# Row sums of the first modulation by column-tiled products, and a re-ordered handover from router to experts

## The chip, the cores and the metric

The kernel runs on one core of one Trainium2 chip. The metric is device time in microseconds (us) of one execution. A core has five engines that are meant here: PE (TensorE, the matrix unit; its weight loads are shown apart as PEld), DVE (VectorE), ACT (ScalarE), POOL (GpSimd) and SP (SyncE, which here only issues DMAs and reads a few integers into registers). Each works through its own instructions in order; they wait for each other on semaphores.

## The reference

Two layers on x of 512 tokens by 1024 channels (f32). Each layer has a token mixer (layer 0: an mLSTM, layer 1: differential attention) and a mixture of experts, each behind a normalisation whose scale and shift come from a vector c:

```python
c_act = silu(c)
for l in range(2):
    mod = c_act @ w_ada[l] + b_ada[l]                 # 1024 -> 6 * 1024
    sh1, sc1, g1, sh2, sc2, g2 = split(mod, 6)
    h = rms(x, norm1[l]) * (1 + sc1) + sh1
    y = mlstm(h) if l == 0 else diff_attention(h)     # first step: h @ w_in
    x = x + g1 * y
    h = rms(x, norm2[l]) * (1 + sc2) + sh2
    x = x + g2 * grouped_moe(h)
```

`grouped_moe` routes each token to one of 4 groups of 4 experts and to the two best experts in it; an expert is 1024 -> 2 x 512, silu(gate) * up, 512 -> 1024. The weights of all 16 experts of a layer are 100 MB in f32.

## The kernel before

Everything is written for a scheduler that is given the instructions in program order and orders each engine's stream by a simulated time; a tile belongs to a tag of a pool with so many buffers, and a new tile of that tag waits until an old one is read for the last time. Two such tags matter: `whi` (3 buffers) and `wlo` (2 buffers) hold the high and low parts into which `split` (line 218) cuts weights, the high part written by ACT, the low part by DVE or POOL. Products that must be exact are made of three products of such parts (`triple`).

**Start.** x is loaded and normalised (`normed_T`). The first two of the six parts of `mod` (shift and scale of layer 0) are made in halves of 512 columns by `ada_half(hf, where)` (line 272). For each of the two parts it loads two blocks of w_ada (128 partitions x 4 x 512, 1 MiB each); ACT multiplies two of a block's four row groups by their column of c, DVE multiplies and adds the others (lines 283 to 289). `sums` then turns the 128 x 512 sums with PE, reduces them with DVE along the free axis (`column_sums`, line 258) and adds b_ada. The first half's result lets `modulated(xT, h, 0)` write h for the first four of eight row groups, and so starts the products of q (`proj_cols`, `strip`), which need `split` weights qk0s0, qk0s2 for the first half and qk0s4, qk0s6 for the second. The second half (`rest_of_h`, line 491) is woven into the first steps of q. Other parts of `mod` are made later, block by block, on ACT and POOL (`ada`, line 237); they share four load buffers (tag `raw`) with the mixer's weights.

**Router.** For each tile t of 128 tokens `tile_done` (line 1009) has POOL multiply x by a row (two pieces of 512 columns), ACT sum its squares, and `rstd_of` (line 317) make the reciprocal root of the mean square, a power, on POOL. `turn` and `logits` make the router's logits on PE; `rows` finishes the normalised rows on DVE and stores them to DRAM from POOL's queue. `choose`, `place` and `order` pick the experts, the place of each token in its expert's list, `count`, the rank of the 13 dynamic experts by count (`rk`), how many blocks are past the planned room (`past`), and `ids`, the experts in rank order. `weigh` has PE make the gates per slot (`psg`), and `by_rank` (line 1137) permutes lists and gates by rank.

**Handover and experts.** `moe` (line 1239) gathers expert 0's rows (`rows_in`, an indirect DMA on POOL), then `overflow` (line 1455) holds a loop over `past` blocks; with these inputs it makes no trip, but all engines go through its entry and exit together. Behind it the rows of expert 0 are turned on PE, written as parts xh and xl by ACT and DVE, and `gate_up` cuts each weight block and multiplies. Experts 0 to 8 run on up to 128 rows with `triple`, the last seven on 64 rows in plain f32 with two column groups of PE side by side (line 1275). The weights come through 15 buffers; the first 14 (layer 0) or 15 (layer 1) loads are issued ahead of the loop. A load for a dynamic expert has its address from a register that SP reads from `ids` (line 1215).

## Time and profile before

| | us |
|---|---|
| median of 3 runs | 1259.03 |
| lowest, highest | 1256.88, 1259.57 |
| profiled execution, own time | 1258.35 |
| its span | 1256.4 |

| engine | busy us | share of the span |
|---|---|---|
| PE | 1113.8 | 89% |
| PEld | 816.6 | 65% |
| DVE | 873.6 | 70% |
| ACT | 698.2 | 56% |
| POOL | 381.4 | 30% |

The mean granted TensorE clock is 0.93 of full (2.4 GHz; the lower level is 1.2 GHz). In round numbers the span is: start to 33 us, layer 0's mixer to 290, its router to 319, its experts to 590, layer 1's mixer to 948, its router to 978, its experts to the end. A share of busy time is a mean over stages with different limits, so each stage is read by itself: the table by stretches gives busy time of each engine there, the timeline gives each instruction with its start, its length and what its engine waited for. A wait for several things is put down to the last of them.

### The profile page before, as it was taken

To read this page: it belongs to the slowest core of one execution; us is meant where nothing else is said; L and a number is where in the kernel's file an instruction comes from. 1 tells how busy PE (TensorE), PEld (TensorE's weight loads), DVE (VectorE), ACT (ScalarE), POOL (GpSimd) and SP (SyncE) were. 2 spreads that over 40 slices of the span, in tenths; PEclk is the share of its full clock that TensorE was granted. 3 is DMA by queue.
4 is the path that set the end of the run, shared out by engine and by line. 5 is a ranking of instruction groups with operands and counts; after the bars stand their busy time and mean duration, and the time that the engine had idled before them with its cause. 6 is when DMAs were issued, how large, how long until landed. Compare 5 with 4: busy or idle time off the path is not lost. (4 is left out here: it accounts for less than half of the span.)

```text
span 1256.4 us, 16914 instructions
## 1 busy us (share of the span) xinstructions
PE 1113.8 (89%) x5714; PEld 816.6 (65%) x5714; DVE 873.6 (70%) x1622; ACT 698.2 (56%) x1164; POOL 381.4 (30%) x273
## 2 busy tenths in 40 slices
PE   3899999987899999995799999888897999999994
PEld 2577877766777875332688877665576787875331
DVE  6955878887788994006767889795776798993006
ACT  5456675442788884112656666565552788884110
POOL 2544572452211111102351455551332211101100
PEclk7799999997899999998799999897896899999997
DMA  9777662183899999998233335320464799999995
GB/s 349 248 246 282 243 233 101 66 341 143 289 390 383 377 390 365 397 409 272 94 102 117 119 127 175 131 73 1 168 248 167 268 386 375 387 384 366 391 410 202
DMA packets 105196, 320.79 MB, mean 255 GB/s; under 512 B 12674, under 2 KB 25098, under 8 KB 105105
## 3 DMA queue, kind: packets, MB, share of 16 engines
q1 hardware_dynamic: 96272, 298.67, 64.6%
q0 software_dynamic: 8832, 20.99, 4.6%
q8 instruction: 47, 0.77, 0.2%
q14 instruction: 45, 0.36, 0.1%
HBM read 309.66 MB, written 20.45 MB: 263 GB/s over the span
## 5 line engine op out<-in xcount | busy, mean ns | idle before, releaser
L253 POOL TENSOR_TENSOR acc<-acc,ada 128x1024 f32<-128x1024 f32 x58 | 151.0, 2604 | 89.4 <-ACT ada L252 36.7
L1275 PE MATMUL pge<-we,xfe 128*64 128x512 f32 x448 | 103.2, 599 | 2.5 <-DMA we<-in_moe_w_gu_dram 2.5
L1247 POOL DMA_INDIRECT xg<-h2d,lstd x26 | 26.4, 1016 | 235.8 <-PE xTe L380 156.3
L1284 DVE TENSOR_TENSOR acte<-acte,pge 128x256 f32<-128x256 f32 x14 | 5.9, 420 | 125.0 <-ACT acte L1283 125.0
L252 ACT ACTIVATE ada<-ada,cact 128x1024 f32<-128x1024 f32 x58 | 64.7, 1143 | 30.8 <-DMA ada<-in_w_ada_dram 30.7
L1275 PEld LDWEIGHTS pge<-we,xfe 128*64 128x64 f32 x448 | 29.3, 136 | 55.6 <-issue 48.2
L877 ACT ACTIVATE p<-p,mx 128x128 f32<-128x128 f32 (+3 forms) x64 | 35.6, 557 | 42.5 <-DVE mx L876 42.5
L1302 PE MATMUL pye<-we,aTe 128*64 128x512 f32 x224 | 54.1, 624 | 1.7 <-ACT aTe L1291 1.1
L320 POOL TENSOR_TENSOR qrs<-qrs,nhalf 128x4 f32<-128x4 f32 x32 | 36.7, 1151 | 61.2 <-DVE qrs L319 47.8
L870 PE MATMUL s<-kTb,qTb 64*128 64x128 f32 (+3 forms) x128 | 44.8, 530 | 11.1 <-DVE mx L873 10.4
L465 POOL TENSOR_TENSOR wo<-wo,grow 128x1024 f32<-128x1024 f32 x16 | 40.1, 2523 | 30.2 <-DVE wos102l L222 15.1
L1302 PEld LDWEIGHTS pye<-we,aTe 128*64 128x64 f32 x224 | 16.4, 144 | 36.5 <-issue 31.9
L873 DVE CUSTOM_DVE_ANT_0 p<-s,maskW 128x128 f32<-128x128 f32 (+3 forms) x64 | 29.8, 484 | 12.6 <-PE s L870 5.5
L1283 ACT ACTIVATE acte<-pge 128x256 f32<-128x256 f32 x14 | 5.4, 384 | 54.6 <-PE pge L1275 54.6
L1333 PE MATMUL pcf<-yo,self 64*128 64x512 f32 x64 | 18.9, 636 | 17.6 <-DVE acte L1284 15.9
L1314 ACT ACTIVATE yo<-pye,twins 128x512 f32<-128x512 f32 x10 | 6.9, 687 | 48.7 <-PE pye L1302 48.7
L1315 POOL DMA_INDIRECT yd<-yo,rows x10 | 10.0, 998 | 78.1 <-ACT yo L1314 77.5
L844 DVE TENSOR_TENSOR qrow<-qrow,qrs 128x256 f32<-128x256 f32 x32 | 26.5, 828 | 7.9 <-POOL qrs L320 7.6
L1291 ACT ACTIVATE aTe<-aTe 128x256 f32<-128x256 f32 x14 | 5.4, 383 | 45.5 <-PE aTe L1289 45.5
L1398 POOL DMA_INDIRECT yd<-yoe,lstd x12 | 14.7, 1225 | 52.4 <-ACT yoe L1503 50.7
L320 POOL TENSOR_TENSOR ors<-ors,nhalf 128x2 f32<-128x2 f32 (+1 forms) x12 | 12.0, 999 | 58.9 <-DVE ors L319 25.0
L250 DVE SCALAR_TENSOR_TENSOR acc<-ada,cact,acc 128x1024 f32<-128x1024 f32 x12 | 15.4, 1281 | 19.4 <-POOL acc L253 16.5
(2545 smaller groups left out, 3963.2 us busy)
## 6 DMA issues: line engine op xcount, KB each, us to landing
we<-in_moe_w_gu_dram SPq DMA_DIRECT2D x128, 1024.0 KB, 9.4
we<-in_moe_w_down_dram SPq DMA_DIRECT2D x64, 1024.0 KB, 10.5
ada<-in_w_ada_dram SPq DMA_DIRECT2D x48, 1024.0 KB, 5.2
yk<-yd SPq DMA_DIRECT2D x16, 512.0 KB, 10.0
wo<-in_a_w_out_dram SPq DMA_DIRECT2D x4, 1024.0 KB, 4.9
wo<-in_b_w_out_dram SPq DMA_DIRECT2D x4, 1024.0 KB, 6.2
x<-in_x_dram SPq DMA_DIRECT2D x4, 512.0 KB, 5.2
qk0w<-in_a_w_in_dram SPq DMA_DIRECT2D x2, 1024.0 KB
```

The lines of the kernel that those rows point to most:

```text
L252: A.activation(raw[:, k], raw[:, k], AF.Copy, scale=cact[:, kt:kt + 1])
L253: G.tensor_tensor(acc, acc, raw[:, k], op=ALU.add)
L320: G.tensor_tensor(r, r, nhalf[:, 0:ncol], op=ALU.pow)
L465: G.tensor_tensor(raw[:, k], raw[:, k], grow, op=ALU.mult)
L844: V.tensor_tensor(row3, row3, r[:, :, None].to_broadcast([P, ng, BHD]), op=ALU.mult)
L870: T.matmul(ps[:, 0:n], part(qTs, h)[q0:q0 + BHD, j * P:(j + 1) * P], part(kTs, h)[q0:q0 + BHD, 0:n], start=True, stop=True)
L873: V.tensor_tensor_reduce(p[:, 0:n], ps[:, 0:n], maskW[:, S - n:S], scale=1.0, scalar=NEG, op0=ALU.add, op1=ALU.max, accum_out=mx[:, cc:cc ...
L877: A.activation(p[:, 0:n], p[:, 0:n], AF.Exp, scale=0.125, bias=mx[:, cc:cc + 1], accum_out=mx[:, 2 + cc:3 + cc])
L1247: G.indirect_dma_start(out=xg[0:n], out_offset=None, in_=h2d[:, :], in_offset=bass.IndirectOffsetOnAxis(ap=itok[0:n], axis=0), bounds_chec ...
L1275: T.matmul(pgu[hf * CS:(hf + 1) * CS].rearrange("p (g c) -> p g c", g=2), x[:, kt], w[:, :, hf], start=kt == 0, stop=kt == NK - 1))
L1302: T.matmul(py[hf * CS:(hf + 1) * CS], aT[:, k, ch * CS:(ch + 1) * CS], w[:, 0, hf * 512:(hf + 1) * 512], start=ch + k == 0, stop=ch + k == 2))
L1333: ordered(T.matmul(banks[hf], sel[at, t], yo[at], start=first, stop=last))
```

## The change

Five edits. (1) `ada_half` no longer scales and adds on ACT and DVE: a zero-padded copy of c (`cpad`, 128 x 8 x 32, in a buffer of tag `wlo`) is the weight of 128 x 32 f32 products, four for each block on four column groups of PE, summed in one PSUM tile over both blocks; the 128 x 512 result is copied out (once by DVE, once by ACT) and its four useful rows are summed by one-column products with a column of ones. (2) In `tile_done` the square and the power come first; the first POOL product of a tile is issued behind the power of the tile before, the second behind its own. (3) `by_rank`, now with the making of `ids` and the add of the second `psg`, is called behind the overflow loop and after the gather of expert 1's rows; `cols`, `rank` and `byrank` move to a pool that lives on. (4) The first two weight splits of expert 0 are made ahead of the loop. (5) The loop's body uses plain f32 products, without splitting weights.

```diff
+    cpad = wsp.tile([P, NK, 32], F32, tag="wlo", name="cpad", bufs=N_LO)
+    V.memset(cpad, 0.0)
+    V.tensor_copy(cpad[:, :, 0], cact)
...
     def ada_half(hf, where):
-        accs = []
+        rows = []
         for i, j in enumerate((1, 0)):
-            acc = room[0].tile([P, D], F32, tag="acc", name=f"acc0{j}{hf}", bufs=2)
-            accs.append(acc)
+            ps = (y_tile, t_tile)[hf](f"rowada{j}{hf}")
             for ch in range(2):
                 raw = load(wk(w_ada[0, ch * 512:(ch + 1) * 512, j * D + hf * 512:j * D + (hf + 1) * 512]), 4, 512,
                            f"ada0{j}{hf}{ch}", where[2 * i + ch])
-                c = [cact[:, ch * 4 + k:ch * 4 + k + 1] for k in range(4)]
-                for n in range(2):
-                    A.activation(raw[:, n] if ch else acc[:, n * 512:(n + 1) * 512], raw[:, n], AF.Copy, scale=c[n])
-                if ch:
-                    V.tensor_tensor(acc, acc, raw[:, 0:2].rearrange("p a n -> p (a n)"), op=ALU.add)
-                for n in range(2):
-                    part = acc[:, n * 512:(n + 1) * 512]
-                    V.scalar_tensor_tensor(part, raw[:, 2 + n], c[2 + n], part, op0=ALU.mult, op1=ALU.add)
-            V.tensor_tensor(acc[:, 0:512], acc[:, 0:512], acc[:, 512:], op=ALU.add)
+                for k in range(4):
+                    T.matmul(ps[k * 32:(k + 1) * 32], cpad[:, ch * 4 + k], raw[:, k], start=ch == 0, stop=ch == 1)
+            row = room[0].tile([P, 512], F32, tag="acc", name=f"row0{j}{hf}", bufs=2)
+            if i:
+                A.activation(row, ps, AF.Copy)
+            else:
+                V.tensor_copy(row, ps)
+            rows.append(row)
         def sums():
-            cs = small.tile([P, 2, 4], F32, tag="cs", name=f"cs0{hf}", bufs=2)
-            column_sums(cs, accs[::-1], f"psada0{hf}")
+            ps = t_tile(f"psada0{hf}")
+            for i, row in enumerate(rows[::-1]):
+                for k in range(4):
+                    T.matmul(ps[:, i * 4 + k:i * 4 + k + 1], row[:, k * P:(k + 1) * P], ones_f[:, 0:1], start=True,
+                             stop=True)
...
     def rstd_of(src, ncol, count, name, pows=[]):
-        G.tensor_tensor(r, r, nhalf[:, 0:ncol], op=ALU.pow)
+        pows.append(G.tensor_tensor(r, r, nhalf[:, 0:ncol], op=ALU.pow))
...
         def tile_done(t):
+            ss = small.tile([P, 1], F32, tag="ss", name=f"sse{l}{t}", bufs=4)
+            A.activation(xT.rearrange("p k t -> p (k t)"), xt[t], AF.Square, accum_out=ss)
+            before = pows[-1:]
+            rst[t] = rstd_of(ss, 1, D, f"re{l}{t}", pows)
             for n in range(2):
                 cols = slice(n * 512, (n + 1) * 512)
-                G.tensor_tensor(h2[:, cols], xt[t][:, cols], arow[:, cols], op=ALU.mult)
-            ss = small.tile([P, 1], F32, tag="ss", name=f"sse{l}{t}", bufs=4)
-            A.activation(xT.rearrange("p k t -> p (k t)"), xt[t], AF.Square, accum_out=ss)
-            rst[t] = rstd_of(ss, 1, D, f"re{l}{t}")
+                with tc.issue_after((pows[-1] if n else before[0]).ins) if n or before else nullcontext():
+                    G.tensor_tensor(h2[:, cols], xt[t][:, cols], arow[:, cols], op=ALU.mult)
...
          def order():
-            later(1, lambda: by_rank(perm, work[:, 2 * N2:5 * N2]))
...
-        def by_rank(perm, moved):
+        def by_rank(work):
+            V.tensor_tensor(sg, sg, held[0], op=ALU.add)
...
             V.tensor_tensor(perm, rk[:, None, :].to_broadcast(square), eidx[:, 0:ND, None].to_broadcast(square),
                             op=ALU.is_equal)
             V.tensor_tensor(turned, perm[0:1], eidx[0:1, None, dyn].to_broadcast([1, ND, ND]), op=ALU.mult)
             V.tensor_reduce(idf, turned, axis=AX.X, op=ALU.add)
             V.tensor_copy(ids, idf)
...
-                    hi, lo = split(raw(k), 1, D, f"gus{nm}{kt}")
+                    hi, lo = ready.pop(0) if ready else split(raw(k), 1, D, f"gus{nm}{kt}")
...
                 def product(ps, xs, w):
                     for kt, x in enumerate(xs):
                         raw = part(w, kt)
                         for n in range(2):
+                            T.matmul(ps[n], x, raw[:, n * 512:(n + 1) * 512], start=kt == 0, stop=kt == len(xs) - 1)
...
         rows_in(0)
+        ready = [split(fetch.ready[0][:, k:k + 1], 1, D, f"guse0{k}") for k in range(2)]
         overflow()
         fetch.more(N_LAST[l], lst[:, 0, 0:1])
         cur = start("e0")
         for hf in range(2):
             turn(cur, xgs[0], hf, "e0")
         rows_in(1)
+        by_rank(yo_tile("work"))
         gate_up(cur, weights, (0, 1), "e0")
```

## Rows read from the trace of the kernel before

**Rows 1.** The page: busy tenths of PE, granted clock, 40 slices of 31.4 us.

```profile
PE   3899999987899999995799999888897999999994
...
PEclk7799999997899999998799999897896899999997
```

**Rows 2.** Stretches: length, busy us (instructions) by engine, clock, DMA share, GB/s.

```profile
13.00:34.00 21.00, 3.00 (x13) 2.37 (x14) 18.32 (x27) 11.10 (x18) 5.34 (x3) 0.57 1.05 388
60.00:230.00 170.00, 163.62 (x772) 131.24 (x771) 122.04 (x222) 103.79 (x161) 81.10 (x36) 1.00 0.59 205
350.00:400.00 50.00, 50.00 (x234) 40.17 (x233) 46.15 (x46) 41.92 (x50) 6.12 (x6) 1.00 1.02 390
```

**Rows 3.** Timeline of the start: start, length (us), engine, line, operation, [idle before, releaser].

```profile
20.98 1.33 ACT L283 ACTIVATE ada<-ada,cact 128x512 f32<-128x512 f32 x2 [1.36 <-DMA ada<-in_w_ada_dram]
...
24.83 2.40 POOL L222 TENSOR_TENSOR qk0s0l<-qk0w,qk0s0h 128x1024 fp32r<-128x1024 f32 x1 [12.67 <-ACT qk0s0h L221]
...
27.83 1.97 PE L264 MATMUL psada<-ident,acc 128*128 128x128 f32 x8 [14.22 <-DVE acc L289]
...
31.72 0.15 DVE L295 TENSOR_TENSOR mod<-cs,vcol 128x8 f32<-128x8 f32 x1
...
33.58 2.08 PE L432 MATMUL qk0p<-ah,qk0s0h 128*128 128x512 f32 x4 [3.77 <-ACT ah L356]
```

**Rows 4.** Timeline, second half of the first modulation and of q.

```profile
40.25 1.06 ACT L221 ACTIVATE qk0s4h<-qk0w 128x1024 fp32r<-128x1024 f32 x1 [1.56 <-DMA qk0w<-in_a_w_in_dram]
...
48.09 1.03 PE L264 MATMUL psada<-ident,acc 128*128 128x128 f32 x8
...
54.72 2.07 PE L432 MATMUL qk0p<-ah,qk0s4h 128*128 128x512 f32 x4 [3.15 <-ACT ah L356]
...
60.40 0.40 PE L432 MATMUL qk0p<-ah,qk0s4h 128*128 128x512 f32 x1
```

**Rows 5.** Timeline, where full-width products give way to column groups of 64.

```profile
479.56 0.40 PE L230 MATMUL pue<-guse87l,xh1e 128*128 128x512 f32 x1
...
479.80 0.39 PE L230 MATMUL pue<-guse87h,xl1e 128*128 128x512 f32 x1
...
480.12 1.94 PE L1275 MATMUL pge<-we,xfe 128*64 128x512 f32 x8
```

**Rows 6.** Timeline, handover in layer 0.

```profile
308.64 1.86 PE L1170 MATMUL psg<-shares,hot 128*128 128x16 f32 x8 [2.36 <-DVE past L1129]
...
313.10 0.06 DVE L1457 MEMSET trip<- 128x1 f32 x1
...
315.66 1.97 PE L380 MATMUL xTe<-ident,xg 128*128 128x128 f32 x8 [2.86 <-POOL we L213]
...
317.08 1.23 DVE L222 TENSOR_TENSOR guse00l<-we,guse00h 128x1024 fp32r<-128x1024 f32 x1 [3.92 <-SPq L1215]
...
318.85 0.58 ACT L382 ACTIVATE xh0e<-xTe 128x512 fp32r<-128x512 f32 x1
...
319.48 0.79 PE L230 MATMUL pge<-guse00h,xh0e 128*128 128x512 f32 x1 [1.85 <-ACT xh0e L382]
```

**Rows 7.** SP's reads of ids, from 305 to 320 us (ns: least/median/most).

```profile
L1215 SPq TENSOR_LOAD <-ids x13: 261/263/274, 309.6 to 319.1; - x13
L1215 SPq FUSED_REGOPS  x13: 147/147/152, 309.9 to 319.4; - x13
```

**Rows 8.** Timeline, handover in layer 1.

```profile
971.71 0.06 DVE L1457 MEMSET trip<- 128x1 f32 x1
...
977.73 0.80 PE L230 MATMUL pge<-guse00h,xh0e 128*128 128x512 f32 x1 [0.39 <-ACT xh0e L382]
```

**Rows 9.** Timeline, power and logits of the last tile in layer 0.

```profile
296.50 0.54 POOL L320 TENSOR_TENSOR re<-re,nhalf 128x1 f32<-128x1 f32 x1 [0.63 <-DVE rt L1159]
...
296.65 2.72 PE L1037 MATMUL psr<-awr,x2T 128*128 128x16 f32 x12
```

**Rows 10.** Waits of PE from 480 to 580 us: total, times, longest.

```profile
PE pge L1275 <- DMA we<-in_moe_w_gu_dram: 1.2, 2, 0.6
```

More of the change, by code (lines that the diff above doesn't have):

```diff
@@ L1173, in weigh @@
             else:
-                V.tensor_tensor(sg, sg, psg, op=ALU.add)
-        return tile_done, xgs, lst, lstd, ids, gates, rows2, twins, count, exc, past, pk, eid
+                held.append(psg)
+        return tile_done, by_rank, xgs, lst, lstd, ids, gates, rows2, twins, count, exc, past, pk, eid
     def overflow_blocks(pool, count, exc, trip):
@@ L1474, in overflow, with turned @@
-                add_to_tokens(*results(py, *place, "o"), "o", [t_tile] * NT)
+                part = lambda w, kt: load(
+                    wk(w[l, ds(er, 1), kt * P:(kt + 1) * P, :].rearrange("o k n -> (o k) n")),
+                    1, D, f"wo{kt}", (pool, "yo", 3))[:, 0]
+                def turned(src, tag):
+                    ps = t_tile("To")
+                    for k in range(4):
+                        T.transpose(ps[:, k * P:(k + 1) * P], src[:, k * P:(k + 1) * P], ident)
+                    x = pool.tile([P, 4, P], F32, tag=tag, name="o" + tag)
+                    A.activation(x, ps.rearrange("p (k t) -> p k t", k=4), AF.Copy)
+                    return [x[:, k] for k in range(4)]
@@ new lines, in product @@
+                def product(ps, xs, w):
+                    for kt, x in enumerate(xs):
+                        raw = part(w, kt)
+                        for n in range(2):
+                            T.matmul(ps[n], x, raw[:, n * 512:(n + 1) * 512], start=kt == 0, stop=kt == len(xs) - 1)
+                    return ps
+                xs = turned(xgs[1][:, 0:512], "xh0") + turned(xgs[1][:, 512:], "xh1")
+                act = activate((None, *product([mm_tile("pgo"), mm_tile("puo")], xs, moe_w_gu)), "o")
@@ new lines, in overflow @@
+                py = product([y_tile("py0o"), y_tile("py1o")], turned(act, "ahi"), moe_w_down)
+                gate, token = place
+                sel = small.tile([P, NT, P], F32, tag="sel", name="selo", bufs=1)
+                yo = yo_tile("o")
+                for n in range(2):
+                    V.scalar_tensor_tensor(yo[:, n * 512:(n + 1) * 512], py[n], gate, grow[:, n * 512:(n + 1) * 512],
+                                           op0=ALU.mult, op1=ALU.mult)
+                for t in range(NT):
+                    V.tensor_scalar(sel[:, t], slot, float(t * P), token, op0=ALU.add, op1=ALU.is_equal)
+                    for n in range(2):
+                        ps = t_tile(f"pco{t}{n}")
+                        T.matmul(ps, sel[:, t], yo[:, n * 512:(n + 1) * 512], start=True, stop=True)
+                        x = xt[t][:, n * 512:(n + 1) * 512]
+                        V.tensor_tensor(x, x, ps, op=ALU.add)
```

51 lines of the change are left out of this document (12 added, 39 removed).

## The prediction

> **What bounds the kernel now.** The profiled execution took 1258.35 us, its span 1256.4; the 1.95 us around the span are kept, and the sum is made against 1258.35, which is 0.7 us under the median of the three runs, 1259.03. The page's slices come first [rows 1]: PE is far from full in slice 1, and the granted clock is below full in slices 1 and 2 and, among others, in 10 and 11 (about 283 to 345 us) and in 31 and 32. The table by stretches [rows 2] then says what sets each stage. From 13 to 34 us PE works 3.00 of 21 us at a mean clock of 0.57, while DMA is full at 388 GB/s. From 60 to 230 us PE is busy 96% at full clock with DMA at 0.59, so what reaches PE earlier moves all of that stage. At 350 to 400 us (big experts) PE is busy 50.00 of 50 us with DMA at 1.02: the experts move as a whole if both products and weight stream start earlier. So PE waits at two kinds of place: the start, and the handover from router to experts, once in each layer. The timeline of these says who is late, and there the change works.
>
> **Start, first half of the modulation.** Today four blocks of w_ada are scaled and added on ACT and DVE, then turned by PE and reduced. The fourth block is there at 20.98 (ACT waited for it), PE turns the sums at 27.83, mod is written at 31.72, the first q product starts at 33.58 [rows 3]. The change removes for both halves 16 ACT scalings, 16 DVE multiply-adds, 8 adds and 16 PE transposes with their reduces; it adds 32 f32 products of 32 columns, four row copies and 16 one-column products. No row shows groups of 32 columns. The nearest are of 64: eight in 1.94 us at full clock, 0.243 each, in pairs on the two halves of the array [rows 5]. So the last block's four cost 0.97 at full clock and 1.9 at half, and half is nearly what this stretch grants [rows 2]. Bounds: 0.5, if all four run at once at full clock, and 3.9, singly at half; I take 1.9, the row's own pattern. For the row copy I take 0.7 (ACT's pass over 512 columns out of PSUM is 0.58 [rows 6]), for the column sums 1.5 (eight transposes are 1.97 [rows 3], and half of the sums can go ahead), for the add and the handshakes 0.6: mod at 20.98 + 1.9 + 0.7 + 1.5 + 0.6 = 25.7. From mod to the first product 1.86 us stay: 27.5, six us earlier. The q weights' low part then matters: POOL ends it at 27.23 [rows 3], just in time. The pad's two DVE steps come at about 3 us, ahead of all this: 0.
>
> The Trainium skill, in TensorEngine Tiling (Array Packing), Theoretical Speedup, gives 32 columns up to four times the speed. By that rule a block would cost 0.5 at full clock and the sum below would be some 2.5 us better (0.9 on the last block, 1.6 on PE in the second half); the trace shows pairs only, and the sum goes by them.
>
> **Start, second half.** Today its sums are late on DVE and are turned on PE at 48.09, behind all first-half products; PE then waits for the new h until 54.72 and returns at half clock until 60.40, though ACT had the weights at 40.25 [rows 4]. After the change no DVE chain is in it. PE: start 27.5; the 48 first-half products keep their 14.5 us (33.58 to 48.09); 16 row-sum products add 16 x 0.243 = 3.9, the column sums 1.1: 47.0. The second half follows at full clock: the 13 products that now take 54.72 to 60.40 take 13 x 0.24 = 3.1, the eight gate products between the halves 1.9: 52.0 where it is 60.40 today, 8.4 us. PE gets a new wait: a row sum waits for its block, and q products are queued behind it. If all of them are held, q starts when the last block lands, about 20.98 + 5 x 1.05 MB at 388 GB/s = 34.5, and the second half still follows at once: gain 3. If PE has full clock throughout, 11. The padded c holds one of the two buffers of tag wlo until the last row sum, so the second low part is split at 35 us at the earliest; PE needs it at about 37: 0, or 3 if PE is faster. PE has little idle time up to 230 us; I give back 0.4: **8 us**, between 3 and 11.
>
> **Powers first.** For the last tile the power now ends at 297.04, while choose() waits for PE's logits, which end at 299.37 [rows 9]: nothing is gained on the path. On POOL the second modulating product now waits for ACT's square and DVE; queued behind it are the row stores and the gather. It ends some 2 us later, the gather comes only after the list, much later: 0, with bounds of 0.5 either way.
>
> **Handover.** Today DVE enters the loop only after the permutation, at 313.10, and PE does its first turn at 315.66, 2.56 later. ACT then loads its table and splits weights before it gets to xh0e at 318.85; the first product is at 319.48 [rows 6]. The loop makes no trip, no line of its body has a row: the plain body saves only code that is jumped over, 0 to 1 us, taken at 0. After the change by_rank and the add of psg stand behind the loop and two splits before it. PE still computes psg before the loop, 308.64 to 310.50, and psg keeps its bank until DVE has added it; so entry cannot be much before 310.7, 2.4 earlier. With ACT free, a turn and xh0e need about 2 us instead of 3.82: 1.8, together 4.2. Against it: two DVE splits of 1.23 [rows 6] lie in DVE's chain of small steps with its short gaps: 0 to 2.5, taken as 1. Net 3.2 in layer 0, bounds 0 and 5. In layer 1 again 2.4 (trip at 971.71), but the first product is there at 977.73 already [rows 8], so 0.4 for ACT, less 1: 1.8, bounds 0 and 4.
> Behind the loop go by_rank's steps, 2.6 us of DVE (310.50 to 313.10) and one more for ids, ahead of the later splits; DVE idles 3.92 us there today [rows 6]. Its PE product twins is queued ahead of expert 0's, and DVE's next splits behind its reading of that. SP's 13 reads of ids, 0.263 + 0.147 each [rows 7], 5.3 us, are mostly ahead of the loop today; behind them on SP are then weight loads. The first load that needs an id is the seventeenth, and its buffer comes free some 5 us after expert 0's first product, at about 320; DVE is out of the loop 2.5 after 310.7, ids is there five small steps later, at about 314.7, the reads end at about 320: 0, up to 2 if ids is late. Handover **5 us**, bounds 0 and 9. Next late is then the low part from DVE, and towards the end of the experts the weights, for which PE waits 1.2 us today [rows 10].
>
> **Sum.** 1258.35 - 8 - 0 - 5 = 1245.
>
> **The rivals.** (1) The handover brings nothing: the splits delay the chain by what leaving out by_rank saves, or by_rank is ordered ahead of the loop after all because psg's bank is wanted there. For it: DVE's gaps in that chain are short. Against: its 2 us wait for psg is free. 1258.35 - 8 = 1250. (2) The start brings little, since row sums hold PE's queue as above: 1258.35 - 3 - 4 = 1251. (3) Slower: PE pays for the row sums where it is the bound. A 64-column product started 0.32 behind a full-width one, against 0.24 between two of a kind [rows 5]; if each of the second half's 16 goes out alone among q products, singly at half clock (0.97) with two changes of width (0.1 to 0.4 each), they cost 16 x 1.5 = 24 us in place of 3.9, against 13 won: 1258.35 + 20 - 13 = 1265. It decides from about 1.1 us per product. The Trainium skill, on the same page, Key Properties, says that a change of tiling mode drains TensorE, which speaks against the change; the row shows 0.1 us for one. (4) The gain is taken back after 60 us, by weight loads that wait for buffers which POOL's adds empty: 1258.
>
> **How the numbers follow.** Forecast 0.50, (1) 0.20, (2) 0.13, (3) 0.07, (4) 0.10. 0.2%, 2.5 us, is about what a measurement of this kernel can tell from no change. Faster 0.50 + 0.20 + 0.13 = 0.83, same 0.10, slower 0.07. The range goes down to 1258.35 - 11 - 9 = 1238, the upper bounds of both places, and up to 1256, which takes in (1) and (2) and both at once (1258.35 - 3).
>
> **What would show it.** Right: first q product near 27.5 us, no gap of PE between the halves of q, the point of today's 60.40 near 52; trip set about 311 and expert 0's first product about 315.3, both less the start's shift; the experts' stage as long as before. Wrong: q products broken up by waiting row sums; 32-column products more than 0.25 us apart at full clock; DVE splits in the middle of choose(); DMA idle behind the loop for late ids; PE waiting for weights between 50 and 230 us.

## The result and the profile after

The changed kernel took 1245.24 us (median; 1234.66 to 1247.03), the kernel before on the same occasion 1258.01 (1256.88 to 1259.57): a ratio of 0.9876, 95% interval 0.9827 to 0.9926. Run five times more beside the kernel before (e1 below) it took 1242.11 against 1259.75: 0.9851, interval 0.9829 to 0.9873. So the change is worth 13 to 18 us. The profiled execution took 1246.32, its span is 1244.4.

The page's busy tenths of PE and the granted clock, to be laid beside [rows 1]:

```profile
PE   6999899987999999995699999888897999999994
PEclk8999999996999999997799999897897999999997
```

PE's share of slice 1 is up, and the stretch around slices 10 and 11 is still below full clock, though PE starts the experts sooner in it.

The timeline of the start in the changed kernel (start, length in us, engine, line, operation, idle time before and who ended it), to be laid beside [rows 3]:

```profile
20.57 1.06 PE L285 MATMUL rowada<-ada,cpad 128*32 128x512 f32 x8 [1.55 <-DMA ada<-in_w_ada_dram]
21.70 0.60 ACT L288 ACTIVATE row<-rowada 128x512 f32<-128x512 f32 x1 [8.59 <-PE rowada L285]
22.35 1.95 PE L297 MATMUL psada<-ones_f,row 128*128 128x1 f32 x16 [0.72 <-ACT row L288]
24.34 0.17 DVE L300 TENSOR_TENSOR mod<-psada,vcol 128x8 f32<-128x8 f32 x1 [7.24 <-PE psada L297]
24.40 2.35 POOL L225 TENSOR_TENSOR qk0s0l<-qk0w,qk0s0h 128x1024 fp32r<-128x1024 f32 x1 [12.67 <-ACT qk0s0h L224]
24.53 2.24 DVE L357 TENSOR_SCALAR a<-mod 128x4 f32<-128x4 f32 x1
28.27 2.07 PE L438 MATMUL qk0p<-ah,qk0s0h 128*128 128x512 f32 x4 [0.25 <-ACT ah L362]
```

PE now waits for the blocks themselves and works the last one off in 1.06 us. (A block is four f32 products; the trace has two records for each, hence x8.) The modulation mod is there at 24.34 instead of 31.72. Then a step of DVE over four columns takes 2.24 us, and the first q product starts at 28.27, 5.31 us earlier. The second half, beside [rows 4]:

```profile
36.64 1.07 PE L285 MATMUL rowada<-ada,cpad 128*32 128x512 f32 x8
44.53 1.84 PE L297 MATMUL psada<-ones_f,row 128*128 128x1 f32 x16
48.77 1.20 PE L438 MATMUL qk0p<-ah,qk0s4h 128*128 128x512 f32 x4 [0.53 <-ACT ah L362]
52.05 0.40 PE L536 MATMUL psg<-al,wg 128*16 128x512 f32 x1
```

The row sums stand between q products with no wait, PE waits 0.53 us between the halves instead of 3.15, and the fourteenth product of the second half, which stood at 60.40, starts at 52.05 (counted from 48.77 as before from 54.72; in the new order it is one of the gate). The handover in layer 0, beside [rows 6], and the same three marks in layer 1, beside [rows 8]:

```profile
289.29 1.09 PE L1034 MATMUL x2T<-ident,x 128*128 128x128 f32 x8 [1.52 <-DVE x L459]
306.01 0.13 DVE L1135 CAST past<-npast 1x1 int32<-1x1 f32 x1
308.15 0.06 DVE L1443 MEMSET trip<- 128x1 f32 x1
311.05 1.97 PE L386 MATMUL xTe<-ident,xg 128*128 128x128 f32 x8 [2.97 <-POOL we L216]
312.20 0.60 ACT L388 ACTIVATE xh0e<-xTe 128x512 fp32r<-128x512 f32 x1 [0.39 <-PE xTe L386]
312.85 0.79 PE L233 MATMUL pge<-guse00h,xh0e 128*128 128x512 f32 x1
...
956.88 0.13 DVE L1135 CAST past<-npast 1x1 int32<-1x1 f32 x1
959.03 0.06 DVE L1443 MEMSET trip<- 128x1 f32 x1
963.24 0.80 PE L233 MATMUL pge<-guse00h,xh0e 128*128 128x512 f32 x1
```

From the count of overflow blocks (past) to expert 0's first product it takes 6.84 us in layer 0 and 6.36 in layer 1; before, 11.06 and 10.70 (past at 308.42 and 967.03).

If the same product is looked up in both profiles, its start before less its start after is the lead. The lead does not simply grow. In the first profile of the changed kernel it is 8.35 us at the first product of qk1 (70.38 before), 3.18 at 177 us, 4.10 at the last product of the out projection, 6.96 when the experts run steadily, 11.65 at the second out projection, 12.86 at the second set of experts. A fall of 5 us in layer 0's attention and a rise of 5 in layer 1's were in no step of the prediction. The experiments began there.

### The profile page after: what moved, and what is told of

It is laid out like the page before. It is cut to its first block, busy times and chain, and to the rows that moved or that the text cites. A ratio compares the mean times of both kernels' runs of the same rounds, so it can differ in the third digit from the quotient of the medians.

```text
span 1244.4 us, 17033 instructions
## 1 busy us (share of the span) xinstructions
PE 1126.9 (91%) x5794; PEld 822.4 (66%) x5794; DVE 857.6 (69%) x1598; ACT 687.6 (55%) x1148; POOL 378.5 (30%) x273
## 4 chain that ended last, share of the span: by engine, by line
PE 41%; DVE 19%; issue 18%; DMA 11%; POOL 5%; ACT 4%; SPq 0%; POOLq 0%; DVEq 0%; ACTq 0%
PE po L233 7%; DMA ada<-in_w_ada_dram 5%; PE pge L233 4%; PE pue L233 4%; PE pge L1284 3%; DMA yk<-yd 2%; PE py0e L233 2%; PE py1e L233 2%; PE pye L1311 2%; POOL acc L256 2%; DVE qrow L850 1%; ACT ada L255 1%; PE s L876 1%; PE psr L1046 1%; DMA xg<-h2d,lst 1%
## 5 line engine op out<-in xcount | busy, mean ns | idle before, releaser
L876 PEld LDWEIGHTS s<-kTb,qTb 64*128 64x128 f32 x128 | 16.3, 201 | 18.7 <-DVE mx L879 10.9
```

Of the source, the lines that this page charges most:

```text
L876: T.matmul(ps[:, 0:n], part(qTs, h)[q0:q0 + BHD, j * P:(j + 1) * P], part(kTs, h)[q0:q0 + BHD, 0:n], start=True, stop=True)
```

## The experiments

**e1, the changed kernel again.** No edit.

> The changed kernel itself, five times more. In its first profile the q product of layer 0 ends 8.35 us earlier than before, but only 2.97 us of that are left at 178 us: at 147 us VectorE's split of v1s2 took 3.40 us (1.21 before) beside three adds of GpSimd in a row, TensorE waited 2.43 us for it and then ran eight products at half clock. Theory A, the coincidence is a matter of the single execution (where the DMA-paced adds of GpSimd fall against the splits): the times spread as the first four did, 1234 to 1247, by 6 us or more, and a profile without the 3.40-us split has kept 7 us or more at 178 us. Theory B, the order of the instructions fixes it: the times lie within 3 us of 1245, as those of the kernel before lie within 3 us of 1258, and the profile shows the 3.40-us split again.

Measured: 1242.11 us (1239.05 to 1243.82), ratio 0.9851 (0.9829 to 0.9873). Two rows from the first profile of the changed kernel, then the same two from this one: DVE's split of v1s2, and PE's product that waits for it.

```profile
143.89 3.40 DVE L225 TENSOR_TENSOR v1s2l<-v1w,v1s2h 128x1024 fp32r<-128x1024 f32 x1
147.35 0.74 PE L414 MATMUL v1p<-v1s2l,ah 128*128 128x512 f32 x1 [2.43 <-DVE v1s2l L225]
```

```profile
140.68 3.43 DVE L225 TENSOR_TENSOR v1s2l<-v1w,v1s2h 128x1024 fp32r<-128x1024 f32 x1
144.16 0.50 PE L414 MATMUL v1p<-v1s2l,ah 128*128 128x512 f32 x1 [1.24 <-DVE v1s2l L225]
```

Neither theory holds whole. The five times spread by 4.8 us, less than A asked, and two of them, 1239.05 and 1239.46, lie lower than B allowed. The stretched split is there again, so it is no accident of the first profile. But it costs 1.24 us here and no drop of the clock (granted 1.00 from 143 to 160 us, 0.90 in the first profile), and 6.35 us of lead are left at 177 us. The price is a matter of the execution.

**f1, the kernel before again.** No edit.

> The kernel before itself, once more, for a second profile. Theory A, the single profile of before that all leads are read against is one draw among several: in it VectorE's split of v1s2 at 148.79 took 1.21 us, where it took 3.40 to 3.43 in six other profiles, also in the two with the old start (148.44 and 148.71), and these two stood 2.6 to 2.9 us ahead of it at the first product of qk1 and 1.4 to 1.6 behind it at 178 us with the same work up to there. So marks of this second profile differ from the first by up to 3 us, both ways, and the gain of the start is to be read against the three old starts together. Theory B, the first profile is typical: all marks up to 290 us lie within 0.5 us of it, and the changed start loses 5 us between 62 and 178 us by a fault of its own. Layer 1: if the growth of the lead there (4.0 to 6.9 us between expert 0's last down products and the second out projection in eight profiles, 0.65 in one) is a draw of the first profile too, that stage is 4 us shorter in this one; if it belongs to the edits, it has the first profile's length within 1 us.

Measured: 1259.58 us, ratio 1.0004 (0.9991 to 1.0018). The second half of q, a wait of PE in qk1 and the same split in this profile of the kernel before:

```profile
54.25 1.20 PE L432 MATMUL qk0p<-ah,qk0s4h 128*128 128x512 f32 x4 [3.16 <-ACT ah L356]
57.52 0.39 PE L432 MATMUL qk0p<-ah,qk0s4h 128*128 128x512 f32 x1
...
75.20 0.50 PE L432 MATMUL qk1p<-ah,qk1s0h 128*128 128x512 f32 x1 [2.17 <-ACT qT L602]
...
148.28 3.43 DVE L222 TENSOR_TENSOR v1s2l<-v1w,v1s2h 128x1024 fp32r<-128x1024 f32 x1
151.76 0.50 PE L408 MATMUL v1p<-v1s2l,ah 128*128 128x512 f32 x1 [1.67 <-DVE v1s2l L222]
```

Theory A for layer 0. The product that stands at 60.40 in [rows 4] stands at 57.52 here: the half clock of the second half of q is in the first profile (granted 0.51 from 53.5 to 60.4 us) and not in this one (1.00). But the time so won is not kept. In f1, e3 and e4 PE then waits 2.2 to 2.3 us for ACT at 75 us (0.21 in the first profile) and has half clock behind that (0.50 in f1 from 76.7 to 80.0 us, 1.00 in the first profile). At 93 us the four profiles of the old start are within 0.9 us of each other again. The short split of the first profile (1.21 us there) was a draw too. The changed start has no fault of its own between 62 and 178 us; the old one meets the same split.

Leads have therefore to be read against several profiles of the same start. The table gives them in us against the first profile of before, which is zero in every row. "New start" are seven profiles whose orders agree up to some 250 us except where the experiment edits them (the first one, e1, e2, e5, e6, e7, f3).

| mark (start in the first profile of before) | old start: f1, e3, e4 | new start | difference of the means, zero counted as a fourth old start |
|---|---|---|---|
| first q product, 33.58 | 0.23, 0.32, 0.12 | 5.31, 4.71, 5.33, 5.40, 5.15, 4.85, 4.69 | 4.9 |
| first product of qk1, 70.38 | 2.86, 2.92, 2.62 | 8.35, 7.71, 7.94, 7.77, 8.70, 7.28, 7.86 | 5.8 |
| last qk1s6h product of qk1, 93.43 | -0.58, -0.73, -0.85 | 7.65, 7.10, 7.28, 7.17, 8.09, 6.63, 7.22 | 7.8 |
| last o0s6h product of o0, 144.97 | 0.61, 0.65, 0.30 | 7.29, 7.78, 8.92, 7.94, 7.36, 6.15, 6.37 | 7.0 |
| first product of o1, 177.16 | -1.16, -1.41, -1.61 | 3.18, 6.35, 7.78, 5.89, 3.29, 3.18, 4.58 | 5.9 |
| last part of the out projection, 288.93 | -0.22, -0.26, -0.49 | 4.10, 7.55, 7.47, 7.01, 4.58, 4.32, 1.84 | 5.5 |

By these marks the start is worth 5 to 8 us: most at 93 us, about 6 from 177 to 290, where single profiles lie between 1.8 and 7.8. In layer 1 the growth of the lead is no draw of the first profile: the stage there is as long in this profile (lead 0.52 behind expert 8, 0.35 at the second out projection). The mark that the expectations call expert 0's down products is the last of dnse8, those of expert 8, at 490 us.

**e2, the row sums alone.** The kernel before with `ada_half` and `cpad` of the change.

```diff
+    cpad = wsp.tile([P, NK, 32], F32, tag="wlo", name="cpad", bufs=N_LO)
...
+                for k in range(4):
+                    T.matmul(ps[k * 32:(k + 1) * 32], cpad[:, ch * 4 + k], raw[:, k], start=ch == 0, stop=ch == 1)
```

> The kernel before with the column-tiled row sums and nothing else. All theories: the first product of qk1 starts near 62.0 (70.38 before). Theory A, the start's gain is partly lost in the attention of layer 0 and what is left runs to the end: at 178 us a lead of 3 us, end near 1258 - 3 to 6 = 1252 to 1255. Rival 1, the lead stays whole: 1250. Rival 2, the lead is lost altogether: 1257 to 1259.

Measured: 1249.76 us (1246.38 to 1254.53), ratio 0.9923 (0.9899 to 0.9948), 6.5 to 12.7 us faster. The lead in its profile is 7.94 at qk1, 7.78 at 177 us, 6.24 at the end of layer 1's out projection: rival 1, it stays. The forecast's 8 us lies inside the interval, the 6 us that the table has from 177 us on just outside its low end. The profiled execution, 1253.78, is the second slowest of the six, so its marks show less than the median does.

**f2, the row sums in one column group.** The same 32 products, one behind the other; the column sums then go over 32 rows.

```diff
-    T.matmul(ps[k * 32:(k + 1) * 32], cpad[:, ch * 4 + k], raw[:, k], start=ch == 0, stop=ch == 1)
+    T.matmul(ps[0:32], cpad[:, ch * 4 + k], raw[:, k], start=ch + k == 0, stop=ch * 4 + k == 7)
```

> The changed kernel with the row sums in one column group: the same 32 products, one behind the other into rows 0 to 31, and column sums over those 32 rows. Theory A, the four groups of a block run side by side (1.06 us a block at full clock): here a block takes 3.4 to 3.9 us at full clock and twice that at half; the four blocks of the second half stand where TensorE bounds, 4 x 2.6 = 10 us, those of the first half outlast the 2.6 us between two blocks' arrivals and cost 4 to 15 more: 1242 + 14 to 25 = 1256 to 1267, at or above the kernel before. Rival, the groups run one behind the other already and the tiling is only a layout: a block takes 1.1 us at full clock here too, and the time is 1242 +- 2.

Measured: 1261.87 us (1257.81 to 1269.43), ratio 1.0026 (1.0005 to 1.0046): slower than the kernel before. Four blocks of the first half, the first q product, and two blocks of the second half:

```profile
14.35 13.92 PE L285 MATMUL rowada<-ada,cpad 128*32 128x512 f32 x32
...
39.50 1.20 PE L438 MATMUL qk0p<-ah,qk0s0h 128*128 128x512 f32 x4
...
45.27 7.05 PE L285 MATMUL rowada<-ada,cpad 128*32 128x512 f32 x16
```

A block costs 3.5 us (13.92 / 4, 7.05 / 2) where it cost 1.06 in four groups: the groups do run side by side, and without them the start's gain is more than eaten up. A product alone takes 0.87 us (13.92 / 16; the 32 records are 16 products). The Trainium skill, in TensorEngine Tiling (Array Packing), Theoretical Speedup, gives up to four times for 32 columns; the trace agrees up to the tail of the last product, 3.3 times.

**e3, the handover alone.** The changed kernel with the old `ada_half` and without `cpad`.

> The changed kernel with the first modulation halves computed as before: powers first, permutation behind the loop and plain loop body remain. Theory A, the handovers carry what the trace shows between the end of each out projection and the experts' steady products, 2.85 us in layer 0 and 2.4 us in layer 1: 1258 - 5.3 = 1253, and the lead is 0 (within 0.5 us) until 290 us. Rival, the handovers carry all that the start didn't keep (12 less 3): 1249. Rival 2, their gain depends on the earlier start: 1256 to 1258.

Measured: 1250.57 us (1246.91 to 1256.73), ratio 0.9940 (0.9917 to 0.9964). Leads: -0.26 at the end of the first out projection, 2.88 at the steady experts, 2.56 behind expert 8, 7.33 at the second out projection, 7.72 at its end, 12.32 at the second experts. Theory A on both handovers, with more in layer 1 (4.6); and, with the old start, again a rise of 4.8 us between expert 8 and the second out projection. Here 4.0 of it come ahead of layer 1's attention (6.54 at the last turn of its x, 602.88 in the first profile of before), and the attention itself, which this run has in yet another order, gives 0.8. The profiled execution, 1247.61, is the second fastest of eight that go up to 1256.73: its marks show more than the median does. By its time the handover is worth 4.5 to 10.5 us.

**e4, the plain body alone.** The kernel before with the loop body of the change (its split operands gone).

```diff
...
-                gate_up(cur, lambda ch: part(moe_w_gu, ch), (0, 1, 2, 3), "o")
-                py = project_down(*act_T(activate(cur, "o"), "o"), lambda ch: part(moe_w_down, ch), "o")
-                add_to_tokens(*results(py, *place, "o"), "o", [t_tile] * NT)
+                xs = turned(xgs[1][:, 0:512], "xh0") + turned(xgs[1][:, 512:], "xh1")
+                act = activate((None, *product([mm_tile("pgo"), mm_tile("puo")], xs, moe_w_gu)), "o")
+                py = product([y_tile("py0o"), y_tile("py1o")], turned(act, "ahi"), moe_w_down)
...
```

> The kernel before with the plain body of the overflow loop and nothing else; the loop makes no trip on these inputs. In the order of ScalarE's instructions this alone moves three splits of the first expert from behind the loop to the end of the out projection. Theory A: the experts' first product follows the loop's start by 1.7 us less in each layer (4.70 us in the changed kernel, 6.38 before), and the two splits of VectorE between the last residual adds cost 1 to 2 us of it in each layer: 1258 - 0 to 3 = 1255 to 1258. Rival, the body carries the handover's gain alone: 1253. The start of the trip counter (313.10 before) moves by less than 2 us under the first, since the permutation still lies ahead of it.

Measured: 1250.87 us (1248.53 to 1255.28), ratio 0.9933 (0.9910 to 0.9956): more than theory A allowed. The handover in layer 0:

```profile
310.65 0.13 DVE L1129 CAST past<-npast 1x1 int32<-1x1 f32 x1
315.34 0.06 DVE L1434 MEMSET trip<- 128x1 f32 x1
319.06 0.60 ACT L382 ACTIVATE xh0e<-xTe 128x512 fp32r<-128x512 f32 x1 [0.84 <-PE xTe L380]
319.71 0.80 PE L230 MATMUL pge<-guse00h,xh0e 128*128 128x512 f32 x1
```

From the trip counter to the first product it takes 4.37 us (6.38 before), in layer 1 3.79 (6.02): theory A on the mechanism. In ACT's order the three first weight splits stand ahead of the loop here (from 285.90 us on; from 316.00 before), though nothing in the program puts them there. The reason is read from the program and not tested by itself: the old body used the tags `whi` and `wlo`, and with them out of the body those splits have nothing to wait for. The leads of the two handovers are 0.57 and 2.28 us; the larger part of the gain, 5.64 us, is in layer 1's attention. A part of that can be read. In before, f1, e2 and e5, all with the old body, PE waits there for two low parts that DVE makes, 0.4 to 0.5 and 1.5 us; the longer wait, from before:

```profile
644.88 0.39 PE L408 MATMUL bv0p<-bv0s4l,bh 128*128 128x256 f32 x1 [1.55 <-DVE bv0s4l L222]
```

Here and in the first profile of the changed kernel, e1, e7, f2, f3 and f4, all with the plain body, PE waits for neither. That is 2.0 us.

**e5, the changed kernel with the old body.** The loop body is that of before (the lines that e4 removes), and the list of early splits is empty.

```diff
-        ready = [split(fetch.ready[0][:, k:k + 1], 1, D, f"guse0{k}") for k in range(2)]
+        ready = []
```

> The changed kernel with the overflow loop's body of before (split operands); powers first, row sums and permutation behind the loop remain, the list of two early splits is empty. The three first splits of ScalarE then lie behind the loop again, and in the attention of layer 1 TensorE, ScalarE and VectorE have the order of the kernel before. Theory A, most of the handover's gain came with the plain body, and much of it not at the handover but by the other order of layer 1's attention: between expert 0's down products of layer 0 and the out projection of layer 1 the lead grew by 4.7 to 5.6 us in three profiles with the plain body and by 0.65 with the old one; here it grows by less than 1.5, the move of the permutation adds 0 to 2, and the time is 1247 to 1250 (the sums alone gave 1249.8). Rival, the permutation's move is worth 2.2 us or more in each layer whatever the body: 1245 or less. Rival 2, the growth in layer 1 follows from the earlier handover: it is there again, 4 us or more.

Measured: 1248.26 us (1245.19 to 1250.79), ratio 0.9906 (0.9887 to 0.9925).

```profile
301.16 0.13 DVE L1135 CAST past<-npast 1x1 int32<-1x1 f32 x1
303.31 0.06 DVE L1466 MEMSET trip<- 128x1 f32 x1
310.10 0.58 ACT L388 ACTIVATE xh0e<-xTe 128x512 fp32r<-128x512 f32 x1
310.76 0.79 PE L233 MATMUL pge<-guse00h,xh0e 128*128 128x512 f32 x1
```

The time is in theory A's range, but its reason falls: from expert 8's down products to the second out projection the lead grew by 4.73 us although PE and ACT have the order of the kernel before in that stage. DVE enters the loop early (2.15 us from past to the counter), and ACT, with its three splits behind the loop, gives 1.1 us of that gain of 2.5 back: 7.45 us from the counter to the first product, where 6.38 stood. This run leaves out body and list together. What speaks against the list is e4, which has none and three splits ahead of the loop all the same, and the changed kernel, whose list names two splits and which has three there. The changed kernel without the list alone was not run.

**e6, the permutation ahead of the loop**, plain body kept.

```diff
+        by_rank(yo_tile("work"))
         overflow()
...
-        by_rank(yo_tile("work"))
```

> The changed kernel with the permutation's sums ahead of the overflow loop again, the plain body kept. At each handover: the trip counter's start comes 2 to 4.6 us later after the count of overflows than in the changed kernel (308.15 less 306.01 there, 313.10 less 308.42 before), and so does the experts' first product. Theory A, the permutation behind the loop is worth this: 1242.1 + 2 x 2.2 = 1246.5, if layer 1's attention, whose order of instructions this edit also changes, takes the same time. Rival, the first product waits for ScalarE's table load and the gathered rows, not for the counter: 1242 to 1243.5.

Measured: 1247.02 us (1245.99 to 1248.14), ratio 0.9895 (0.9873 to 0.9916).

```profile
304.33 0.13 DVE L1135 CAST past<-npast 1x1 int32<-1x1 f32 x1
306.84 0.06 DVE L1443 MEMSET trip<- 128x1 f32 x1
312.20 1.97 PE L386 MATMUL xTe<-ident,xg 128*128 128x128 f32 x8 [2.86 <-SPq L1224]
314.00 0.80 PE L233 MATMUL pge<-guse00h,xh0e 128*128 128x512 f32 x1
```

Theory A in size, by another way than it said: the counter is set early here too (2.51 us behind past), but PE's first turn behind the loop is released by SP's reads of ids, which stand ahead of the loop, and the first product comes 9.67 us behind past in layer 0 and 9.13 in layer 1. The edit also changes the order in layer 1's attention, as was expected, so the 5 us by which this run is slower than e1 need not all lie at the handovers.

**e7, the powers last.** The changed kernel with `tile_done` of before: h2's products ahead of square and power.

> The changed kernel with the products of h2 ahead of square and power in each router tile, as before; ScalarE's order stays the same. Forecast by the prediction: no difference, within 0.5 us in a trace, so 1240 to 1245 here. Rival, the power of the last tile comes earlier in the changed kernel and the router with it: 1 to 3 us slower, 1243 to 1246, to be seen between the last product of the out projection and the first router score of the last tile.

Measured: 1241.68 us (1237.31 to 1246.98), ratio 0.9868 (0.9842 to 0.9894): no difference, as forecast.

**e8, layer 0's later modulation on DVE.**

```diff
-                elif k == 0 and l == 0:
+                elif l == 0:
```

> The changed kernel with all modulation products of layer 0 behind the first halves as multiply-adds on VectorE (16 of 1.28 us more there, 16 scalings of 1.1 us less on ScalarE and 16 adds of 2.4 us and more less on GpSimd). Theory A, what is lost of the start's lead between 62 and 178 us (5.4 us in the first profile of the changed kernel, 1.3 in the second) is the collision of GpSimd's adds with VectorE's splits and scans, which take 2.3 to 3.4 us in place of 1.2 beside them: no split in this stretch takes over 2 us, the lead of 8 us is kept, 1238 to 1241, and the times lie closer together. Rival, VectorE is short of time there (45 of 60 us busy in two stretches): 20 us more of its own work costs more than the collisions, 1244 to 1255.

Measured: 1244.17 us (1241.72 to 1246.46), ratio 0.9870 (0.9850 to 0.9890).

```profile
147.37 1.21 DVE L225 TENSOR_TENSOR v1s2l<-v1w,v1s2h 128x1024 fp32r<-128x1024 f32 x1
148.64 0.80 PE L414 MATMUL v1p<-v1s2l,ah 128*128 128x512 f32 x1 [2.67 <-DVE v1s2l L225]
```

The rival: this split takes 1.21 us now, but comes so late in DVE's queue that PE waits 2.67 us for it; the lead is already down to 2.27 at qk1. As a whole the run is level with the changed kernel.

**f4, three of seven products of the modulation that runs at 135 to 164 us on DVE.**

```diff
-                elif k == 0 and l == 0:
+                elif k == 0 and (l == 0 or j == 0):
```

> The changed kernel with three of the seven accumulating products of layer 1's first modulation column (they run between 135 and 164 us) as multiply-adds on VectorE, as all columns of layer 0 have it; GpSimd has three adds less there. Theory A, the run of two or three adds of GpSimd at 141 us is what stretches VectorE's split of v1s2 to 3.4 us and sets TensorE waiting 0.9 to 2.4 us, at times with the clock halved behind it: the split takes 1.2 to 2.4 us, the lead at 178 us is 6 to 8 us in place of 3.2 and 6.4, and the time is 1239 to 1241. Rival, VectorE's three products of 1.28 us cost as much: 1242 to 1244.

Measured: 1248.49 us (1245.39 to 1254.27), ratio 0.9927 (0.9901 to 0.9954).

```profile
142.12 1.21 DVE L225 TENSOR_TENSOR v1s2l<-v1w,v1s2h 128x1024 fp32r<-128x1024 f32 x1
144.36 0.39 PE L414 MATMUL v1p<-v1s2l,ah 128*128 128x512 f32 x1
...
186.69 1.23 PE L663 MATMUL n<-va,sT 128*128 128x257 f32 x2 [2.38 <-DVE sT L646]
210.80 1.23 PE L663 MATMUL n<-va,sT 128*128 128x257 f32 x2 [2.94 <-ACT core L666]
```

Theory A on the cause: with fewer adds on POOL the split takes 1.21 us, PE does not wait, and 8.30 us of lead stand at 177 us. The rival on the time: 8.7 us are lost between 177 and 218 us, where the edit has also changed the order of PE's products and PE waits for DVE and ACT. That POOL's adds stretch the split and make PE wait is so shown; an edit that keeps the gain was not found.

**f3, the first low part of the q weights on DVE.**

```diff
-    yield k0 + k, split(raw[:, k:k + a], a, n, f"{name}s{k0 + k}", G if name in ("qk0", "b00") else V)
+    yield k0 + k, split(raw[:, k:k + a], a, n, f"{name}s{k0 + k}", G if name in ("qk0", "b00") and (name, k0, k) != ("qk0", 0, 0) else V)
```

> The changed kernel with one instruction on another engine: the first low part of the q weights (qk0s0l, GpSimd, 2.35 us at 24.40) on VectorE, ahead of the first modulation. Nothing else in any engine's order changes. Theory A, the 128x4 step behind the modulation took 2.24 us in place of 0.15 because GpSimd's split ran beside it: here the split takes 1.2 us, the step 0.15 to 0.2, and the first q product comes 0.5 to 1.2 us earlier, 1241 to 1242. Rival, the step's 2.24 us are a wait of its own (for the modulation's write or the scale row): it takes over 2 us again, the split's 1.2 us come on top, and the first q product is 1 us later.

Measured: 1241.19 us (1237.04 to 1249.45), ratio 0.9862 (0.9832 to 0.9892). The small step in this profile; the column sums and the step in e1, which has the split on POOL; POOL's split and the step in e5:

```profile
27.23 0.17 DVE L357 TENSOR_SCALAR a<-mod 128x4 f32<-128x4 f32 x1
```

```profile
23.39 3.58 PE L297 MATMUL psada<-ones_f,row 128*128 128x1 f32 x16 [0.72 <-ACT row L288]
27.20 0.17 DVE L357 TENSOR_SCALAR a<-mod 128x4 f32<-128x4 f32 x1
```

```profile
24.31 2.36 POOL L225 TENSOR_TENSOR qk0s0l<-qk0w,qk0s0h 128x1024 fp32r<-128x1024 f32 x1 [12.62 <-ACT qk0s0h L224]
25.99 0.70 DVE L357 TENSOR_SCALAR a<-mod 128x4 f32<-128x4 f32 x1
```

Between this run and e1 nothing is decided. In both, PE stood at half clock in the start (granted 0.50 from 22 to 28 us; the column sums took 3.57 and 3.58 us, 1.95 in the first profile), mod came at 27.00 to 27.02, POOL's split was over, and the step takes 0.17 in either. But the rival falls: the 2.24 us are no wait of the step's own.

The other profiles decide for the collision. Where the step starts while POOL's split runs, it ends 0.02 to 0.03 us behind it, however long that takes: 2.24 us in the first profile (split to 26.75, step from 24.53 to 26.77), 0.59 to 0.70 in e2, e5, e7 and e8. Where the split is over, it takes 0.17.

## Why the prediction was right, step by step

The forecast's time and its two places were right. That the first measured gain, 12.8 us (9.3 to 21.8 by its interval), meets the forecast sum of 13 so closely is luck: run again, the gain is 17.6, with 16.0 to 21.5 by the interval, which leaves 13 outside. The price of a block came right by two errors that cancel, one term of the handover was too small, and what runs on from layer 1 was not in the sum.

**First half of the start.** The last block takes 1.06 us at full clock and 1.94 at half (taken: 1.9), the copy 0.60 (0.7), and mod is there at 24.34 in one profile and 27.00 in the other (25.7). The column sums were under-sized: 1.95 and 3.58 us instead of 1.5. The first q product starts at 28.27 and 28.87 where 27.5 stood; the mean lead there is 4.9 us instead of 6.

**The price of a block: right by luck.** The prediction took the x8 of [rows 5] for eight products, 0.243 us each. The page of before has the same line of the program over the whole run:

```profile
L1275 PE MATMUL pge<-we,xfe 128*64 128x512 f32 x448 | 103.2, 599 | 2.5 <-DMA we<-in_moe_w_gu_dram 2.5
```

The program makes 16 of these products for each of seven experts in two layers, 224 in all, and the row has 448: two records for each product. The row thus prices four products, in pairs, at 1.94 us at full clock and 3.9 at half, twice what was taken. Against that, four groups of 32 run all at once and not in pairs, which halves the price again: 1.06 and 1.94. The same holds for the 3.9 us that 16 products were to cost PE in the second half: three blocks stand among the q products at 1.06 or 1.07 each, and the fourth, 1.93 at half clock, comes ahead of the first q product (26.09). The 0.5 us a block that the prediction worked out by the rule on 32 columns carries the same error. With the 0.87 us that f2 shows for a product alone, four at once make 0.87, and the 1.06 from the block's first start to its last end speaks for the rule, not for the pairs by which the sum went.

**Second half of the start.** PE's part came as worked out: the sums at 46.4 (47.0 forecast), the point of 60.40 at 52.05 (52.0). The weak step is on the other side of the subtraction: "returns at half clock until 60.40, though ACT had the weights" was taken as what the kernel does, and in f1, e3 and e4 the same product stands at 57.46 to 57.77, with the loss at 73 to 80 us instead. What the start gains is so a matter of the mark: 5.8 us at 70, 7.8 at 93, 7.0 at 145, about 6 from 177 on, and 6.5 to 12.7 by e2's time. The term of 8 is not refuted. Not in any term were the waits for v1s2 (1.24 us and more with the new start, 1.67 in f1).

**cpad in a wlo buffer.** POOL's second low part starts at 36.89 instead of 27.19, as worked out ("at 35 us at the earliest"), and PE takes other products first: no gap of PE.

**Powers first.** Nothing, as forecast: e7.

**Handover.** Right in size: 2.9 us in layer 0 and 4.2 in layer 1 (means of eight profiles with both edits; 0.2 and 0.8 in the three with neither), so net 6.2 instead of 5. By its terms: from past to the loop's entry 2.5 us less in both layers (2.4 forecast); from there to the first product 1.7 less in layer 0 (1.8 forecast) and 1.8 in layer 1, where 0.4 stood. That is the term that was mis-sized: [rows 8] show neither ACT's table load nor its splits. The 0.4 is about PE's last wait there (0.39), and about what the two layers differ by (6.38 and 6.02); neither says how long ACT keeps xh0e waiting. In layer 1 of before, as in layer 0, a table load (1.28 us at 972.95) and three splits stand ahead of it. The two early low parts cost what was taken, 1: PE waits 1.52 us for the last residual add (0.26 before) behind DVE's split at 287.30. SP's 13 reads run from 313.9 to 321.3 and cost nothing: the lead stays 6.96 from 327 to 485 us.

```profile
L1224 SPq TENSOR_LOAD <-ids x13: 262/262/278, 313.9 to 321.3; - x13
```

**Where the prediction named the wrong part.** It took the plain body at 0 ("saves only code that is jumped over") and gave ACT's gain to the list of early splits. The runs speak for the reverse: with the plain body alone the splits go ahead of the loop (e4), with neither body nor list they stay behind it (e5). The list by itself was not tested. The body was to be judged by what it lets go ahead of it, not by the time of a loop that makes no trip. Nor do the two edits simply add up: from past to the first product the plain body alone saves 2.0 us (e4) and the rest without it 1.5 (e5), both together 4.2; with the old body ACT's three splits use up 1.1 us of the 2.5 that the early entry gives.

**Rivals.** (1) Handover without gain: refuted by e3 and by the link from past to the first product, 6.8 to 7.6 us in the eight profiles with both edits against 11.1 in three with neither (layer 0). Its first half, splits in the middle of the router, is there and costs 1 us. (2) Row sums that hold PE's queue: no wait of PE for a block among the q products. (3) Slower through PE: not with the groups; f2 shows that without them it would have been so, 1261.87. That this is near the 1265 worked out for it says little: that sum priced a product alone at half clock at 0.97 us, and f2 shows 0.87 at full clock. (4) Gain taken back behind 60 us: not by weight loads. Its like is there, POOL's adds against DVE's splits, but for both starts.

**What stays open.** From expert 8's down products of layer 0 to the second out projection the time is 2.9 to 6.9 us shorter in the eleven profiles with an edit at the handover, and -0.2 to 0.7 in the three without (before, f1, e2). It is no effect of the start (e2), and not of PE's and ACT's order in that stage alone (e5 has the old one). In seven profiles 2.0 us of it are the two waits named under e4, and in e3 most of it comes ahead of the attention; what the rest is was not found.

Open too is how the gain divides. By the marks the start gives 6 (5 to 8), the handover 6.2 and that stage about 5, together 17; the last two are 11 of it. By whole times the start alone gives 6.5 to 12.7 (e2) and the handover with all that follows from it 4.5 to 10.5 (e3), at the middle 9.7 and 7.6, again 17. Both sums come near the repeated 17.6, but marks of one profile and times of several runs put up to 4 us on different sides.

And it is open what lets single executions of the changed kernel differ by 12 us (1234.66 to 1247.03) where those of the kernel before mostly stay within 8.

None of the variants is faster than the changed kernel by more than their scatter: e7 and f3, at 1241.7 and 1241.2, are level with it.

## What to carry to other kernels

Before a slow stretch of one profile is put into a sum as a gain, take a second profile of the same kernel: a half-clock stretch was at 53 to 60 us in one and at 77 to 80 in three others. Before a row is divided by its count, ask the program how many products it stands for: here a record was half an f32 product. An edit inside a loop that makes no trip is judged by what the scheduler may now put ahead of the loop. And a forecast total that comes true says little about its terms: here it was the marks along the way, read against several profiles and against the times of the single edits, that showed what was luck, what was too small and what was missing.

## What the runs showed of the hardware

DVE steps can take the length of POOL's instruction beside them. A 128x4 step took 2.24, 0.70 and 0.59 us beside a two-input split of POOL and 0.17 behind it. It ends within 0.03 us of POOL's instruction, so it is held, not slowed. The split v1s2l took 3.39 to 3.48 us beside POOL's adds in eleven profiles: in f1 it starts at 148.28, POOL's add ends at 150.62, and the split ends 1.09 later. It took 1.21 in three. Two of these had adds thinned out (e8, f4). In the third, the first profile of before, the split starts at 148.79, 0.08 us ahead of an add, and it is the add that is long, 3.42 us. The Trainium skill, in SBUF — State Buffer, Who interferes with whom, says that such instructions of VectorE and GpSimd exclude each other for their whole length, whoever comes first; the trace agrees.

Four column groups of 32 in f32 take 1.06 us for four products of 512 columns at full clock, 1.94 at half. In the first profile of the changed kernel they change places with full-width products at little cost: a block starts 0.32 us behind the product before it (33.27 to 33.59), and the second product behind it follows the first by 0.34 (34.59 to 34.93), where 0.23 is usual.
